# Weights kept split in DRAM: staging high and low parts in one layer and recalling them in the next, on one Trainium2 core

## The chip, the cores and the metric

The kernel runs on one core of a Trainium2 chip. The metric is the device time of one execution in microseconds, the median of several executions. The engines are TensorE (PE in the profile; PEld is its weight load), VectorE (DVE), ScalarE (ACT), GpSimd (POOL) and SyncE (SP), which here only issues DMA transfers. Each engine takes its instructions in the order of the program and waits on semaphores for the others. A queue of DMA issues is in order too: an issue that waits holds up those behind it.

## The reference

A decoder trunk of two layers on x of 1024 tokens by 1024 channels, in float32. Layer 0 is a gated pooling mixer, layer 1 a gated sliding-window attention that reads one shared K/V.

```python
for l in range(DEPTH):                                   # DEPTH = 2, N_A = 1
    shift, scale, gate = jnp.split(c_act @ ada_w[l] + ada_b[l], 3, axis=-1)
    if l < N_A:
        h = modulate(rmsnorm(x, norm_g[l]), shift, scale)
        y = pool_mixer(h, a_w_in[l], a_w_group[l], a_scale[l], a_w_out[l])
    else:
        if l == N_A:
            kb, vb = shared_kv_blocks(x, c_act, kv_norm_g, kv_ada_w, kv_ada_b, w_kv)
        h = modulate(rmsnorm(x, norm_g[l]), shift, scale)
        y = swa_sink_mixer(h, kb, vb, pos_bias, mask, b_w_in[j], b_sinks[j], b_w_out[j])
    x = x + gate[:, None, :] * y
return rmsnorm(x, final_g)
```

`pool_mixer` is a projection to u and z, trailing means of u over 2, 4, 8 and 16 tokens, a grouped projection, a gate by silu(z), and the out projection `a_w_out`. `swa_sink_mixer` is a projection to queries and gates (`b_w_in`), attention in blocks of 128 tokens with sinks, a gate, and the out projection `b_w_out`.

## The kernel before

Channels lie on the 128 partitions and tokens along the free dimension, in two halves of 512 tokens (q = 0 and 1). To keep float32 accuracy each matrix product is three passes of TensorE in the rounded type float32r: each operand is split into a high part (the value rounded) and a low part (the value less the high part), and high by high, high by low and low by high are summed in PSUM. A weight tile has 128 x 1024 numbers (512 KB). To split one, SyncE loads it into `raw`, ScalarE casts it to `wh`, and VectorE subtracts to make `wl` (`fetch`, `split_w`, `load_w`, lines 119 to 134). `raw`, `wh` and `wl` are rings of two buffers, so a weight can be split while the one before it is in use, and not earlier.

Layer 0 ends with its out projection (lines 829 to 864): 16 steps through `order`, each with one weight tile of `wao[n, hf]`, which `half_w` loads and splits one step ahead. For n below `LATE` = 5 both token halves are done (48 matmuls a step, steps 0 to 9), for n of 5 to 7 only the first (24 matmuls, steps 10 to 15). Into the steps the program weaves work that has nothing to do with them: `ADA[i]` calls of `ada_step`, each of which loads 512 KB of `ada_rest` into a `tmp` buffer (a ring of three) and takes a dot product on VectorE (line 239). At the end of an n the `residual` (line 686) adds the product to x, and squares are summed (lines 191 and 195). In this part TensorE's order is that of the program; a list scheduler of the language sets the order of the other engines from its own estimates.

The second token half of n = 7, 6, 5 follows (`last_chunk`, line 868) in an order written out by due times (`at`), beside the norm and the modulation of layer 1 (`step_h`, `fold_l`) and the first keys and values. `get_raw`, `take_h` and `take_l` load and split the weights for n = 6 and 5 again, and `wkv` and `wb[0]`.

Layer 1 (from line 989) runs a list of items `specs`: `keys`, `values`, `queries`, `gates`, `out_part`, `out_quarter`. Each names its weight as its first element, and the loop at the end loads and splits the weight for the next item (`load_w`) before it runs the present one. A GEMM here is 24 matmuls. Attention (`attend`, line 1086) is woven in by a clock: scores on TensorE, the softmax on VectorE and ScalarE, transposes (line 1125), two masks by GpSimd (lines 1134 and 1137), and the product with the values `LAGS` = 6 us later. Every weight of `wkv`, `wb` and part 0 of `wbo` is loaded and split twice, once for each token half. Part 1 of `wbo` is also split by `load_last` into four tiles that stay for the last quarter items; its low parts come from GpSimd (line 1224).

Of the kernel before, what the change touches and what calls it, by code (L numbers as in the profile page):

```python
# [18 lines left out]
P = 128  # L19
# [27 lines left out]

ENDS = (0, 1, 3, 5, 7)
# [7 lines left out]
def trunk(ctx, tc, xT, c, pack, ada_first, ada_rest, wu0_in, wg0_in, wa, wg, wao, wkv,  # L56
# [9 lines left out]
    pp = ctx.enter_context(tc.tile_pool(name="psum", bufs=1, space=PSUM))  # L66

# [65 lines left out]
    def load_w(src):  # L133
        return split_w(*fetch(src))

# [82 lines left out]
    with ExitStack() as sa:  # L218
# [580 lines left out]
        with tc.manual_schedule(engines={ET.PE}):  # L799
# [37 lines left out]
            ws, outs = {}, {}  # L837
            ws[0, 0] = half_w(0, 0)
            gather(4, 5, 6, 7)
            for i, (n, hf) in enumerate(order):  # L840
                if i + 1 < len(order):
                    ws[order[i + 1]] = half_w(*order[i + 1])
                if i == 0:
                    gather(8, 9)
                    new_x()
                    again_x(0)
                    gather(10, 11, 12, 13)
                elif i < 8:
                    again_x(i)
# [5 lines left out]
                for _ in range(ADA[i]):  # L855
                    ada_step()
                if hf == 1:
# [4 lines left out]
            assert rest_at[0] == len(rest_cols)  # L862
# [78 lines left out]
        def get_raw(key, src):  # L941
            lraw[key] = fetch(src)[0]

        def take_h(key):
            w = (ws if isinstance(key, tuple) else got)[key] = [
                wp.tile([P, 1024], F32R, tag=t, name=t) for t in ("wh", "wl")]
            nc.scalar.copy(out=w[0], in_=lraw[key])

        def take_l(key):
            w = (ws if isinstance(key, tuple) else got)[key]  # L950
            nc.vector.tensor_sub(out=w[1], in0=lraw.pop(key), in1=w[0].bitcast(F32))

        lraw = {}
        NT = 12 * 0.2157
        nl = 4 * len(late)
        weights = ([((n, hf), wao[n, hf]) for n in late[1:] for hf in range(2)]
                   + [("wk", wkv[0]), ("wv", wkv[1]), ("wq", wb[0])])
        for i, (key, src) in enumerate(weights):
            t = NT * 2 * (i + 1)
# [54 lines left out]
    def keys(q, hk, ps=None):  # L1014
# [11 lines left out]
        return wkv[0], lambda w: gemm_steps(w, 0, hk, KT, done)  # L1026
# [3 lines left out]
    def values(q, hk, ps=None):  # L1030
# [5 lines left out]
        return wkv[1], lambda w: gemm_steps(w, 0, hk, KT, done)  # L1036
# [15 lines left out]
    def queries(q, r, j, h1):  # L1052
# [14 lines left out]
        return wb[2 * r + j], run  # L1067

    def gates(q, r, j, h1):
# [12 lines left out]
        return wb[8 + 2 * r + j], run  # L1082
# [83 lines left out]
    def out_part(q, part, n2):  # L1166
# [11 lines left out]
        return wbo[part, n2], run  # L1178
# [39 lines left out]
    def load_last():  # L1218

        raw = wp.tile([P, 1024], F32, tag="raw", name="raw")  # L1220
        nc.sync.dma_start(raw, wbo[1, len(last_w)])
        w = hp.tile([P, 2, T], F32R, tag="h", name="wo")
        nc.scalar.copy(out=w[:, 0, :], in_=raw)
        nc.gpsimd.tensor_sub(out=w[:, 1, :], in0=raw, in1=w[:, 0, :].bitcast(F32))
        last_w.append((w[:, 0, :], w[:, 1, :]))
# [103 lines left out]
    def woven(l, at):  # L1329

        r = []
        for i, x in enumerate(l):
            r.append(x)
            if i in at:
                r.append(bare(load_last))
        return r

# [16 lines left out]
        *woven(project_out(0, 1) + project_out(1, 0)[:2], (0, 2, 4, 6)),  # L1354
# [8 lines left out]
    with tc.manual_schedule(engines={mybir.EngineType.PE}):  # L1363
        srcs = [i for i, sp_ in enumerate(specs) if sp_[0] is not None]
        loaded = {srcs[0]: got["wq"]}
# [66 lines left out]
```

## Time and profile before

| what | value |
|---|---|
| median of 3 runs | 985.02 us (984.18 to 985.11) |
| profiled execution | 984.87 us |
| its span | 982.6 us |
| TensorE busy | 961.9 us, 98% |
| VectorE, ScalarE, GpSimd busy | 775.7, 458.1, 145.0 us |
| moved by DMA | 125.67 MB, mean 128 GB/s |
| HBM read, written | 111.22 MB, 13.63 MB |

The span runs from the first instruction to the last; the execution's own time is a little longer. A row of the groups reads: line, engine, operation, tile written <- tiles read, shapes and count, then busy us and mean ns of one, then the idle time of the engine just before and who ended it. A row of a window reads: from and to, its length, busy us and count of each engine, the TensorE clock granted (1.00 is full), the mean busy share of the 16 DMA engines, and GB/s.

### The profile page before, as it was taken

What the parts mean: (1) busy time and instruction counts of PE and PEld (TensorE: products, weight loads), DVE (VectorE), ACT (ScalarE), POOL (GpSimd) and SP (SyncE); (2) the same over time, 40 slices, a digit from 0 to 9 for tenths busy, and PEclk for the clock granted to TensorE, in tenths of its full rate; (3) what the DMA queues carried; (4) which work ended last, traced back from release to release, by engine and by line L of the source; (5) the groups of instructions that cost most, each with busy time, mean ns of one, the idle gap of its engine ahead of it and who ended that gap; (6) DMA issues with size and microseconds to landing.
All of it is one profiled execution on the core that took longest, in us unless ns stands there. A gap on an engine that the chain in (4) does not pass through costs nothing.

```text
span 982.6 us, 12696 instructions
## 1 busy us (share of the span) xinstructions
PE 961.9 (98%) x4538; PEld 801.2 (82%) x4538; DVE 775.7 (79%) x1411; ACT 458.1 (47%) x902; POOL 145.0 (15%) x173
## 2 busy tenths in 40 slices
PE   8999999999999999999999999999999999999996
PEld 6788888888888887888888888877888888887786
DVE  5897978677978699676782278599899878889985
ACT  6534434333433244551111145486677546566544
POOL 2100000000000000000000000052324313335723
PEclk9999999999999999999999999999999999999998
DMA  9453622264225411779861223222211221223222
GB/s 331 183 174 114 192 103 65 78 201 150 65 85 194 150 64 57 262 267 327 305 216 65 86 64 130 86 65 69 82 66 64 87 86 65 64 88 106 86 87 86
DMA packets 40625, 125.67 MB, mean 128 GB/s; under 512 B 4465, under 2 KB 6641, under 8 KB 40434
## 3 DMA queue, kind: packets, MB, share of 16 engines
q1 hardware_dynamic: 40416, 123.82, 37.6%
q10 hardware_dynamic: 146, 1.05, 0.3%
q8 instruction: 35, 0.57, 0.2%
q14 instruction: 28, 0.23, 0.1%
HBM read 111.22 MB, written 13.63 MB: 127 GB/s over the span
## 4 chain that ended last, share of the span: by engine, by line
PE 78%; DVE 16%; issue 2%; ACT 2%; POOL 1%; DMA 0%; POOLq 0%; DVEq 0%; SPq 0%; ACTq 0%
PE ps_d L214 14%; PE ps_S L214 9%; PE ps_d L636 9%; PE ps_d L203 6%; PE ps_d L204 6%; PE ps_d L205 6%; PE ps_S L636 4%; PE ps_o L214 4%; PE ps_tp L214 3%; DVE wl L123 2%; PE ps_d L374 2%; PE ps_o L636 2%; PE ps_tp L636 2%; DVE tmp L542 2%; PE ps_tp L1125 1%
## 5 line engine op out<-in xcount | busy, mean ns | idle before, releaser
L121 ACT CAST wh<-raw 128x1024 fp32r<-128x1024 f32 x73 | 76.5, 1048 | 101.4 <-PE ps_d L214 78.5
L123 DVE TENSOR_TENSOR wl<-raw,wh 128x1024 fp32r<-128x1024 f32 x73 | 94.2, 1290 | 26.7 <-ACT wh L121 22.8
L203 PE MATMUL ps_d<-hm,wh 128*128 128x512 f32 x288 | 113.8, 395 | 0.0
L205 PE MATMUL ps_d<-hm,wl 128*128 128x512 f32 x288 | 112.4, 390 | 0.3 <-DVE wl L123 0.3
L204 PE MATMUL ps_d<-hm,wh 128*128 128x512 f32 x288 | 112.4, 390 | 0.0
L239 DVE CUSTOM_DVE_ANT_0 tmp<-tmp,cact,pk 128x1024 f32<-128x1024 f32 x48 | 60.7, 1282 | 33.2 <-DMA tmp<-ada_rest 32.9
L214 PE MATMUL ps_d<-gh,wh 128*128 128x512 f32 x224 | 82.0, 389 | 0.0
L214 PE MATMUL ps_S<-gh,wh 128*128 128x512 f32 x192 | 64.5, 390 | 0.0
L205 PEld LDWEIGHTS ps_d<-hm,wl 128*128 128x128 f32 x288 | 54.1, 188 | 12.6 <-DVE wl L123 1.1
L636 PE MATMUL ps_d<-hs,ws 128*128 128x512 f32 x264 | 63.4, 389 | 0.0
L1115 ACT ACTIVATE pt<-pt,nm 128x129 f32<-128x129 f32 x128 | 50.2, 394 | 26.8 <-DVE nm L1111 24.6
L203 PEld LDWEIGHTS ps_d<-hm,wh 128*128 128x128 f32 x288 | 54.1, 188 | 10.2
L204 PEld LDWEIGHTS ps_d<-hm,wh 128*128 128x128 f32 x288 | 54.2, 188 | 10.0
L636 PEld LDWEIGHTS ps_d<-hs,ws 128*128 128x128 f32 x264 | 49.5, 188 | 10.3
L542 DVE TENSOR_TENSOR tmp<-tmp 128x1039 f32<-128x1039 f32 (+3 forms) x40 | 49.4, 1235 | 6.8 <-ACT tmp L672 5.7
L612 ACT CAST ws<-tw 128x512 fp32r<-128x512 f32 x44 | 26.8, 621 | 53.9 <-PE ps_tp L214 15.1
L636 PE MATMUL ps_d<-ha,ws 128*128 128x512 f32 x216 | 51.9, 389 | 0.0
L534 POOL MEMSET tmp<- 128x16 f32 x16 | 1.7, 111 | 331.4 <-DVE tmp L542 115.9
L214 PEld LDWEIGHTS ps_d<-gh,wh 128*128 128x128 f32 x224 | 42.1, 188 | 8.7
L636 PEld LDWEIGHTS ps_d<-ha,ws 128*128 128x128 f32 x216 | 40.5, 188 | 8.4
L147 POOL TENSOR_TENSOR rs<-v,mhalf 128x4 f32<-128x4 f32 (+1 forms) x7 | 8.2, 1164 | 241.6 <-DVE v L145 241.6
L214 PE MATMUL ps_d<-gh,wl 128*128 128x512 f32 x112 | 43.6, 389 | 0.0
(294 smaller groups left out, 2492.0 us busy)
## 6 DMA issues: line engine op xcount, KB each, us to landing
tmp<-ada_rest SPq DMA_DIRECT2D x48, 512.0 KB, 4.7
raw<-wb SPq DMA_DIRECT2D x32, 512.0 KB, 3.3
raw<-wa SPq DMA_DIRECT2D x28, 512.0 KB, 3.7
raw<-wao SPq DMA_DIRECT2D x20, 512.0 KB, 4.1
ad<-ada_first SPq DMA_DIRECT2D x16, 512.0 KB, 5.0
x<-xT SPq DMA_DIRECT2D x32, 256.0 KB, 5.9
raw<-wbo SPq DMA_DIRECT2D x16, 512.0 KB, 3.3
kept_g<-tmp SPq DMA_DIRECT2D x14, 512.0 KB, 2.9
```

What stands on the lines that cost most here:

```text
L121: nc.scalar.copy(out=wh, in_=raw)
L123: nc.vector.tensor_sub(out=wl, in0=raw, in1=wh.bitcast(F32))
L203: mm(ps, lh, acts(k, 0), start=k == 0, stop=False)
L204: mm(ps, lh, acts(k, 1), start=False, stop=False)
L205: mm(ps, ll, acts(k, 0), start=False, stop=k == n - 1)
L214: mm(p, lhs, acts(k, hl, q), start=start and k == 0 and s == 0, stop=stop and k == n - 1 and s == 2)
L239: nc.vector.tensor_tensor_reduce(out=raw, in0=raw, in1=ca, scale=0.5, scalar=pk[:, bcol:bcol + 1], op0=ALU.mult, op1=ALU.add, accum_out=ad ...
L374: mm(psu[i, q], w0[k // 2][:, k % 2, w, i * P:(i + 1) * P], block(k, q)[hl], start=k == 0 and s == 0, stop=k == KT - 1 and s == 2)
L542: nc.vector.tensor_add(out=nx[:, 2 * s - 1:], in0=cur[:, 2 * s - 1:], in1=cur[:, s - 1:PAD + T - s])
L612: nc.scalar.copy(out=ws[i][:, 0, :], in_=src)
L636: mm(ps, lhs, acts(k, hl), start=start and k == 0 and s == 0, stop=k == 3 and s == 2, skip_group_check=True)
L1115: nc.scalar.activation(pt[:, i, :P + 1], pt[:, i, :P + 1], AF.Exp, bias=nm[:, i:i + 1], scale=-1.0, accum_out=den[:, i:i + 1])
```

## The change

While the out projection of layer 0 runs, 18 weight tiles of layer 1 (both of `wkv`, all 16 of `wb`) are loaded into a `tmp` buffer and split there: the high part goes to one of two `stage` tiles (ScalarE), the low part back into the buffer (VectorE). `keep` then stores both parts to DRAM, through SyncE. `STAGED[i]` says how many are done in step i. The four late output weights (n = 5 and 6) are split as before and kept as well. From then on `recall` brings a pair back by two transfers that GpSimd issues, straight into tiles of the rounded type. `pair_tiles` takes the pair from the two `raw` buffers or one of the two `wh`, `wl` pairs in turn, so three pairs rotate, and items of layer 1 have their weight two items ahead. The eight `wbo` tiles are loaded and split once each by `load_out`, with part 0 kept for the second token half and part 1 held on chip; `load_last` and `woven` are gone, and two out items change places.

```diff
+STAGED = (0, 0, 0, 0, 0, 1, 2, 3, 3, 3, 1, 1, 1, 1, 1, 1)
...
+    kp = ctx.enter_context(tc.tile_pool(name="kept", bufs=1, space=bass.MemoryType.DRAM))
...
+    def keep(key, hi, lo):
+        kept_w[key] = [kp.tile([P, 1024], F32, name="kw") for _ in range(2)]
+        for dst, src in zip(kept_w[key], (hi, lo)):
+            nc.sync.dma_start(dst, src.bitcast(F32))
+    def pair_tiles():
+        tags = (("raw", "raw"), ("wh", "wl"), ("wh", "wl"))[turns[0] % 3]
+        turns[0] += 1
+        return [wp.tile([P, 1024], F32R, tag=t, name="w2") for t in tags]
+    def recall(key):
+        w = pair_tiles()
+        for dst, src in zip(w, kept_w[key]):
+            nc.gpsimd.dma_start(dst, src)
+        return w
...
+            staged = [("kv", i, wkv[i]) for i in range(2)] + [
+                ("b", i, wb[i]) for i in (0, 1, 8, 9, 2, 3, 10, 11, 4, 5, 12, 13, 6, 7, 14, 15)]
+            def stage():
+                name, i, src = staged.pop(0)
+                raw = tmp()[:, :1024]
+                nc.sync.dma_start(raw, src)
+                hi = stage_hi[len(staged) % 2].rearrange("p a c -> p (a c)")
+                nc.scalar.copy(out=hi, in_=raw)
+                lo = raw.bitcast(F32R)
+                nc.vector.tensor_sub(out=lo, in0=raw, in1=hi.bitcast(F32))
+                keep((name, i), hi, lo)
...
                     ws[order[i + 1]] = half_w(*order[i + 1])
+                    if LATE <= order[i + 1][0] < KT - 1:
+                        keep(order[i + 1], *ws[order[i + 1]])
...
                 for _ in range(ADA[i]):
                     ada_step()
+                for _ in range(STAGED[i]):
+                    stage()
...
-            at(t - 4 * NT + 1.31 if i > 1 else -1.0, get_raw, key, src)
-            at(t + 0.05, take_h, key)
-            at(t + 1.3, take_l, key)
+        for i, w in enumerate(weights):
+            at(NT * 2 * i + 0.05 if i else -1.0, get_w, *w)
...
+    def load_out(part, n2):
+        raw = bp.tile([P, 1024], F32, tag="raw1", name="raw1", bufs=2)
+        nc.sync.dma_start(raw, wbo[part, n2])
+        if part:
+            t = hp.tile([P, 2, T], F32R, tag="h", name="wo")
+            last_w.append((t[:, 0, :], t[:, 1, :]))
+            w = last_w[-1]
+        else:
+            w = pair_tiles()
+        nc.scalar.copy(out=w[0], in_=raw)
+        nc.vector.tensor_sub(out=w[1], in0=raw, in1=w[0].bitcast(F32))
+        if not part:
+            keep(("o", part, n2), *w)
+        return w
+    def load_any(key):
+        return recall(key) if key in kept_w else load_out(*key[1:])
...
-        *woven(project_out(0, 1) + project_out(1, 0)[:2], (0, 2, 4, 6)),
+        *project_out(1, 0)[:2],
+        *project_out(0, 1),
...
-                nxt = srcs.index(i) + 1
+                nxt = srcs.index(i) + 2
                 if nxt < len(srcs):
-                    loaded[srcs[nxt]] = load_w(specs[srcs[nxt]][0])
+                    loaded[srcs[nxt]] = load_any(specs[srcs[nxt]][0])
```

The order on SyncE in the out projection. `raw` is a weight of layer 0's out projection, `tmp` from `ada_rest` an ada step, `tmp` from `wb` a stage's load, `kw` a store of a kept part. Before, from the load for step 9 (`raw_3994`) to that for step 15 (`raw_4278`):

```order
L130 DMA raw_3994<-wao 128x1024
L253 DMA tmp_4125<-ada_rest 128x1024
L253 DMA tmp_4167<-ada_rest 128x1024
L253 DMA tmp_4200<-ada_rest 128x1024
L253 DMA tmp_4238<-ada_rest 128x1024
L253 DMA tmp_4271<-ada_rest 128x1024
L130 DMA raw_4062<-wao 128x1024
L130 DMA raw_4136<-wao 128x1024
L130 DMA raw_4170<-wao 128x1024
L130 DMA raw_4207<-wao 128x1024
L130 DMA raw_4241<-wao 128x1024
L130 DMA raw_4278<-wao 128x1024
```

Now, the last 12 of the 19 rows from behind the load for step 12 to that for step 13 (`raw_4335`):

```order
L869 DMA tmp_4278<-wb 128x1024
L145 DMA kw_4228<-stage_3842 128x1024
L145 DMA kw_4229<-tmp_4224 128x1024
L145 DMA kw_4246<-wh_4242 128x1024
L145 DMA kw_4247<-wl_4244 128x1024
L145 DMA kw_4282<-stage_3843 128x1024
L145 DMA kw_4283<-tmp_4278 128x1024
L145 DMA kw_4292<-wh_4288 128x1024
L145 DMA kw_4293<-wl_4290 128x1024
L276 DMA tmp_4320<-ada_rest 128x1024
L869 DMA tmp_4323<-wb 128x1024
L133 DMA raw_4335<-wao 128x1024
```

The weight loads for the last steps stood side by side behind the last ada step; now stage loads, stores and ada steps stand between each two of them.

The order on VectorE at the end of the out projection: `wl` is the low part of a step's weight, `x` a residual, `sqh` the sum of squares, `tmp,adac` a dot, `tmp` with `stage` the low part of a staged weight. Before, from the residual at the end of step 11 (`ps_S_4142`) on, with the weights for steps 13, 14 and 15:

```order
L686 SCALAR_TENSOR_TENSOR x_3426<-ps_S_4142,adac_110,x_3426 128x512
L123 TENSOR_TENSOR wl_4211<-raw_4207,wh_4209 128x1024
L195 TENSOR_TENSOR sqh_3628<-sqh_3628,sq_4204 128x512
L123 TENSOR_TENSOR wl_4245<-raw_4241,wh_4243 128x1024
L686 SCALAR_TENSOR_TENSOR x_3427<-ps_d_4213,adac_110,x_3427 128x512
L123 TENSOR_TENSOR wl_4282<-raw_4278,wh_4280 128x1024
```

Now, from the same residual (`ps_S_4250`), with the weight for step 12 (`wl_4290`):

```order
L709 SCALAR_TENSOR_TENSOR x_3428<-ps_S_4250,adac_112,x_3428 128x512
L262 ISA tmp_4202,adac_112<-tmp_4202,cact_121,pk_75 128x1024
L262 ISA adac_112 128x1
L218 TENSOR_TENSOR sqh_3630<-sqh_3630,sq_4332 128x512
L262 ISA tmp_4205,adac_112<-tmp_4205,cact_121,pk_75 128x1024
L262 ISA adac_112 128x1
L873 TENSOR_TENSOR tmp_4208<-tmp_4208,stage_3842 128x1024
L126 TENSOR_TENSOR wl_4290<-raw_4286,wh_4288 128x1024
L873 TENSOR_TENSOR tmp_4216<-tmp_4216,stage_3843 128x1024
L873 TENSOR_TENSOR tmp_4224<-tmp_4224,stage_3842 128x1024
```

The split for step 13 stood behind the residual of step 11, and now that for step 12 stands there, with dots and a stage's subtraction ahead of it. Behind these rows come a dot, a stage, a dot and a stage, and then the split for step 13; the residual of step 13 and one stage more stand ahead of the split for step 14.

More of the change, by code (lines that the diff above doesn't have):

```diff
@@ L856, in trunk @@
                     ada_step()
+                if STAGED[i] and not stage_hi:
+                    stage_hi += [slot("stage") for _ in range(2)]
+                for _ in range(STAGED[i]):
+                    stage()
                 if hf == 1:
@@ L1177, in run @@
                 yield from gemm_steps(w, i * 512, acts, 4, done)
-        return wbo[part, n2], run
+        return ("o", part, n2), run
     def bare(f):
```

46 lines of the change are left out of this document (12 added, 34 removed).

## The prediction

> **What bounds the kernel now.** I read the page's parts 1 and 2 first. They show the share of each engine and the 40 slices of the span, 24.6 us each.
>
> ```profile
> span 982.6 us, 12696 instructions
> PE 961.9 (98%) x4538; PEld 801.2 (82%) x4538; DVE 775.7 (79%) x1411; ACT 458.1 (47%) x902; POOL 145.0 (15%) x173
> PE   8999999999999999999999999999999999999996
> DVE  5897978677978699676782278599899878889985
> DMA  9453622264225411779861223222211221223222
> GB/s 331 183 174 114 192 103 65 78 201 150 65 85 194 150 64 57 262 267 327 305 216 65 86 64 130 86 65 69 82 66 64 87 86 65 64 88 106 86 87 86
> ```
>
> TensorE is busy in every slice but the first and the last, so an engine relieved of work pays only where TensorE stands idle now, and any new wait of TensorE is paid in full. The DMA row has room in most places, but not in slices 16 to 19 (393 to 491 us). The stretches around the edit, in us of busy time, come next.
>
> ```profile
> core 0: us, PE busy (x) PEld busy (x) DVE busy (x) ACT busy (x) POOL busy (x), PEclk, DMA share, GB/s
> 439.00:507.00 68.00, 68.00 (x302) 56.31 (x301) 46.88 (x72) 10.13 (x12) 0.00 (x0) 1.00 0.88 299
> 507.00:565.00 58.00, 58.00 (x258) 48.02 (x257) 20.40 (x26) 11.06 (x13) 0.00 (x0) 1.00 0.26 87
> 565.00:640.00 75.00, 74.73 (x358) 62.58 (x357) 55.04 (x93) 36.88 (x63) 4.74 (x6) 1.00 0.28 92
> 640.00:700.00 60.00, 56.21 (x282) 46.54 (x281) 55.89 (x124) 45.85 (x98) 25.68 (x23) 1.00 0.20 64
> 700.00:975.00 275.00, 270.50 (x1433) 230.34 (x1432) 236.92 (x569) 164.72 (x403) 103.15 (x100) 1.00 0.25 81
> 975.00:982.60 7.60, 1.22 (x4) 0.93 (x4) 2.74 (x8) 0.00 (x0) 0.57 (x1) 0.50 0.39 138
> ...
> 5.00:20.00 15.00, 14.78 (x52) 10.57 (x53) 9.85 (x11) 8.81 (x14) 4.64 (x4) 1.00 1.01 362
> ```
>
> From 439 to 565 us TensorE does not idle at all. From 565 to 975 it idles for 0.27 + 3.79 + 4.50 = 8.6 us, and this is all that layer 1 can give back. The waits of TensorE say whom it waits for there, and the groups from 565 us on say what the change takes off those engines.
>
> ```profile
> PE ps_tp L1125 <- DVE pt L1119: 6.1, 5, 1.6
> ...
> L123 DVE TENSOR_TENSOR wl<-raw,wh 128x1024 fp32r<-128x1024 f32 x45 | 60.0, 1334 | 12.2 <-ACT wh L121 9.9 <-PE ps_o L1149 1.7
> L121 ACT CAST wh<-raw 128x1024 fp32r<-128x1024 f32 x45 | 47.0, 1045 | 15.2 <-issue 7.6 <-PE ps_d L204 6.4 <-ACT qt L1062 0.9
> L1134 POOL TENSOR_SCALAR_AFFINE_SELECT prev<-cur 128x1024 fp32r<-128x1024 f32 x28 | 33.3, 1189 | 46.8 <-DVE cur L1129 46.8
> ```
>
> **The gain in layer 1.** Of the 45 splits after 565 us, the eight of wbo stay as loads with a split. The other 37 lose 37 x 1.045 = 38.7 us of ScalarE and 37 x 1.334 = 49.4 us of VectorE. The five softmax waits for VectorE (6.1 us) are the target. At least 0 us is gained if VectorE's other work still arrives late, at most the 8.6 us of idle time. I take 5.0 us, nearer to the 6.1 us of the waits than to the end at nothing, because the wbo splits remain in the final stage. The four split writes of `load_last` that leave GpSimd are worth nothing: its queue has 103 us of work in 275.
>
> **What stages the pairs: the out projection of layer 0.** Its 16 steps start at 423.7 us. Ten steps have 48 matmuls and six have 24.
>
> ```profile
> L214 PE MATMUL ps_o<-gh,wh x64: 389/389/389, 423.7 to 531.6; 128*128 128x512 f32 x64
> 559.01 0.62 PE L214 MATMUL ps_S<-gh,wh 128*128 128x512 f32 x2
> 559.46 0.39 PE L214 MATMUL ps_S<-gh,wl 128*128 128x512 f32 x1
> 559.69 0.62 PE L214 MATMUL ps_S<-gh,wh 128*128 128x512 f32 x2
> ...
> 438.78 0.33 SPq L130 DMA_DIRECT2D raw<-wao  x1
> 507.47 49.42 SPq L130 DMA_DIRECT2D raw<-wao  x8
> ...
> tmp<-ada_rest SPq DMA_DIRECT2D x48, 512.0 KB, 4.7
> raw<-wb SPq DMA_DIRECT2D x32, 512.0 KB, 3.3
> tmp<-kept_g SPq DMA_DIRECT2D x5, 512.0 KB, 5.8
> ```
>
> Three matmuls start every 0.68 us (559.01 to 559.69), 0.227 us each: a step is 10.9 or 5.44 us. So TensorE starts step 12 at 543.4, step 13 at 548.8, step 14 at 554.2 and step 15 at 559.7 us. SyncE issues the load for step 4 at 438.78 us.
>
> Now I count SyncE's transfers in units of 512 KB (0.524 MB), from the load for step 4 up to and with that for step 15. Before: 12 weight loads, 30 of ada_rest and eight halves of x, 46 units. The loads for steps 10 to 15 stood last and alone. After: the same 46, plus 16 stage loads, 30 stage stores and 8 stores of late pairs, 100 units. The queue is in order, and the changed rows have the weight loads scattered between: the cumulative count is 55 at the load for step 11, 69 for step 12, 88 for 13, 95 for 14 and 100 for 15.
>
> At what rate do they go? The two busiest slices moved 331 and 327 GB/s; I take their mean, 329, because both held such long queues of loads: 1.594 us a unit. Its ends: 362 (window 5 to 20 us, share 1.01) and 299 (439 to 507 us, share 0.88, which has the same three-deep ring of tmp buffers). A unit alone lands 3.3 us after issue, so 1.7 us come on top of its 1.6. The split that follows is on ScalarE and VectorE, whose durations in this stage are these.
>
> ```profile
> L121 ACT CAST wh<-raw 128x1024 fp32r<-128x1024 f32 x13 | 13.7, 1055 | 86.2 <-PE ps_d L214 78.5 <-PE ps_S L214 7.7
> L239 DVE CUSTOM_DVE_ANT_0 tmp<-tmp,cact,pk 128x1024 f32<-128x1024 f32 x30 | 37.9, 1283 | 22.8 <-DMA tmp<-ada_rest 22.6
> L123 DVE TENSOR_TENSOR wl<-raw,wh 128x1024 fp32r<-128x1024 f32 x13 | 15.9, 1220 | 12.9 <-ACT wh L121 12.7
> L195 DVE TENSOR_TENSOR sqh<-sqh,sq 128x512 f32<-128x512 f32 x10 | 6.5, 684 | 0.0
> L239 DVE DVE_READ_ACCUMULATOR2_ANT adac<- 128x1 f32 x30 | 2.5, 82 | 0.0
> L191 ACT ACTIVATE sq<-x 128x512 f32<-128x512 f32 x10 | 6.3, 634 | 9.2 <-DVE x L686 8.9
> L686 DVE SCALAR_TENSOR_TENSOR x<-ps_S,adac,x 128x512 f32<-128x512 f32 x3 | 2.2, 749 | 3.3 <-PE ps_S L214 3.3
> ```
>
> In ScalarE's row the split waits 78.5 us for TensorE: the data lie ready and the buffer is what is missing. That is the cover, and this change uses it up. A weight is ready 1.7 + 1.06 + 1.22 = 4.0 us after its turn in the queue. At 329 GB/s:
> step 11: 438.8 + 55 x 1.594 + 4.0 = 530.5, needed at 537.9, in time.
> Step 12: 438.8 + 69 x 1.594 + 4.0 = 552.8, needed at 543.4: TensorE waits 9.4 us.
> Step 13: 583.1; TensorE is free at 552.8 + 5.4 = 558.2: 24.9 us.
> Step 14: 594.2, free at 588.5: 5.7 us. Step 15: 602.2, free at 599.6: 2.6 us.
> Sum 42.6 us. Only step 15 sets it: at 362 GB/s (1.448 us a unit) it is ready at 587.6, 27.9 us late; at 299 (1.753) at 618.1, 58.4 us late.
>
> The added waits on SyncE push the same way. Each store waits for ScalarE's cast or VectorE's subtraction, and the weight load stands behind it; a stage holds its tmp buffer through load, split and store, where an ada step holds it for load and dot. I charge them nothing beyond the rate, since the queue is full either way; they argue against 362. The extra work on ScalarE (18 casts, 19 us) and VectorE (18 subtractions, 22 us) lies in stretches in which VectorE has 37.6 us free after 507 us, so it costs no throughput, but its order does (rival C).
>
> After a stall TensorE may run slow: in the last window, with long pauses, the clock is 0.50. Between nothing and one pass at half speed (5.4 us more in step 15; the earlier ones hide behind the next load) I take nothing, since every other window reads 1.00.
>
> **The recalls.** GpSimd issues 44 pairs. The trace has no transfer from this queue. A pair's buffers come free when the weight three before is finished, two GEMMs or 10.9 us ahead of need. From below a pair costs one landing, 3.3 us; from above, for both together, the slowest median of a 512 KB load (5.8) behind two selects of GpSimd (2 x 1.19): 8.2 us. Nearest is the 5.8 us, since two transfers share the engines; all lie under 10.9, so I charge 0. Without that cover each microsecond over costs up to 44 us in all. The stores of wbo's part 0 (8 units) and the last stages (8 units after step 15) fall where the DMA share is 0.20 to 0.28, and cost nothing. Of a recall that waits for TensorE, GpSimd's selects behind it are queued; TensorE's use of those lies a lag of about 6 us later by the kernel's own table.
>
> **Sum.** The profiled execution took 984.87 us (its span 982.6 and 2.3 around it), 0.15 below the median of 985.02. 984.87 + 42.6 - 5.0 = 1022.5 us.
>
> **The rivals.**
> A, the forecast: 27.9 to 58.4 us of stalls, less 8.6 to 0 us: 1004 to 1043 us. Chance 0.70.
> B, recalls that land late, on top of A. For it: a queue that no row shows, a new kind of write into the rounded type, and a DMA load twice as large in layer 1. Against it: 81 GB/s in that stage, so doubled 162. It decides when a pair takes over 10.9 us; at 12 us, 44 x 1.1 = 48 us more, 1071 us. Chance 0.13.
> The Trainium skill speaks for it: "SBUF — State Buffer", section "SBUF: two separate sides", its box on the "DVE blocks DMA" trap says that GpSimd's cores write the descriptors of such a transfer and cannot do so while VectorE holds the port pair that both share, in copies above all. By that page's section "Who interferes with whom", a subtraction of two tensors, VectorE's main work here, has no such mode; no run so far shows either.
> C, the DMA engines are faster than every row and VectorE's order alone stalls TensorE. Ahead of the low part for step 12 now stand a residual that waits for the end of step 11, two dots with their accumulator reads of 82 ns, an add and a stage: 0.75 + 2 x 1.37 + 0.68 + 1.22 + 1.22 = 6.6 us, less the two matmuls that need only the high part, 0.45: 6.15. For step 13, five subtractions and two dots, 8.8 us, against 5.4 us of matmuls: 3.4. For step 14, residual, square, add, stage and split after the end of step 13: 4.5 - 0.45 = 4.05. Sum 13.6, so 984.87 + 13.6 - 5.0 = 993.5 us. Chance 0.10.
> The Trainium skill gives a ceiling for that: "DMA: Bandwidth & Descriptors", section "Where 436 GB/s comes from", 435 GB/s; by it the load for step 15 would be 3.6 us late (estimate from that page), and C would hold. The trace's 362 stands against it.
> D, the other side: the low-share stretch after 507 us takes the staging and no weight comes late. For it: 58 us at 0.26. Against it: the 54 units more are 28.3 MB, and 58 us x (329 - 87) GB/s has room for 14.0. It decides if the queue reaches step 15 by 555.7 us, 449 GB/s. Then 984.87 - 5.0 = 979.9 us. Chance 0.05.
> E, C without the 4.05 us of step 14, and the whole idle time of layer 1 gained: 984.87 + 9.55 - 8.6 = 985.8 us, no change. Chance 0.02.
>
> **How the numbers follow.** 0.2% is about what a measurement of this kernel can tell from no change. Faster is D, 0.05; same is E, 0.02; slower is A, B and C, 0.93. The time is A's. The range runs from C's 993 to 1050, past A's 1043 by the half-speed pass and rounding; it leaves out D, E and most of B, 0.18 or so.
>
> **What the changed profile would show.** Right: four idle stretches of TensorE between 543 and 605 us, before the first matmuls of steps 12 to 15, the largest at step 13; DMA share at 0.9 from 424 to past 600 us; the softmax waits of layer 1 mostly gone. Wrong if the DMA engines pass 400 GB/s through the stores, if TensorE idles in the middle of layer 1's GEMMs for a recalled pair, or if the weight loads leave SyncE as early as before.

## The result and the profile after

The changed kernel takes 1035.08 us (median of 5 runs, 1033.75 to 1039.28) against 985.11 us of the kernel before on the same chip: a ratio of 1.0507, 95% interval 1.0484 to 1.0531. The profiled execution took 1035.08 us, its span 1033.4. The page of the changed kernel, part 1 and the slices (now 25.8 us each):

```profile
PE 977.4 (95%) x4538; PEld 811.9 (79%) x4538; DVE 740.2 (72%) x1385; ACT 432.5 (42%) x872; POOL 174.2 (17%) x257
PE   8999999999999999999993399998999999999896
DMA  9444421452154116798998875734445544352022
```

In balance VectorE and ScalarE have 35.5 and 25.6 us less work, and TensorE has two slices at 3 tenths. Those slices (542 to 594 us) are the out projection's end, where the DMA row stands at 8 tenths. In stretches:

```profile
core 0: us, PE busy (x) PEld busy (x) DVE busy (x) ACT busy (x) POOL busy (x), PEclk, DMA share, GB/s
424.00:507.00 83.00, 83.00 (x368) 68.73 (x367) 53.09 (x76) 24.32 (x33) 0.00 (x0) 1.00 0.88 315
507.00:543.00 36.00, 36.00 (x161) 29.80 (x160) 20.62 (x26) 10.16 (x12) 0.00 (x0) 1.00 0.94 353
543.00:565.00 22.00, 9.82 (x29) 6.73 (x27) 12.45 (x17) 5.86 (x6) 0.00 (x0) 0.77 0.88 331
565.00:620.00 55.00, 34.54 (x123) 26.82 (x124) 19.02 (x23) 10.80 (x13) 4.39 (x5) 0.72 0.84 317
```

TensorE idles 12.2 us from 543 to 565 and 20.5 us from 565 to 620 us, and its clock falls to 0.77 and 0.72. TensorE's waits follow for two stretches: the out projection and the first of the last chunks (424 to 620 us), and behind the dots layer 1:

```profile
PE ps_d L237 <- ACT wh L124: 27.4, 2, 18.6
PE ps_S L237 <- ACT wh L124: 3.4, 1, 3.4
PE ps_o L165 <- DVE sqh L218: 1.1, 1, 1.1
PE ps_S L237 <- DVE wl L126: 0.7, 1, 0.7
...
PE ps_tp L1156 <- DVE pt L1150: 4.8, 3, 2.7
PE ps_o L165 <- POOL sqh L218: 4.4, 1, 4.4
```

Which part of the program lost how much is read from one instruction that both kernels have 128 times, the first product of the scores in layer 1: from its first start back lies layer 0, from its first to its last start layer 1. Kernel before, then the changed one:

```profile
L1105 PE MATMUL ps_S<-KH,qt x128: 220/282/368, 626.2 to 931.6; 128*128 128x256 f32 x112, 128*128 128x128 f32 x16
```

```profile
L1136 PE MATMUL ps_S<-KH,qt x128: 220/282/563, 671.3 to 983.1; 128*128 128x256 f32 x112, 128*128 128x128 f32 x16
```

The first score comes 45.1 us later, 0.5 of which stood before the out projection began. Layer 1 between the two is 311.8 us long instead of 305.4, 6.4 us more. Behind the last score 0.7 us are saved, which makes the 50.8 us of the spans. (Kernels that share the layer 0 of the kernel before reach the first score at 625.9 to 628.3 us in the traces below, and this difference already stands before the out projection. So the length from first to last score is the better measure of layer 1 in what follows.)

**The out projection, step by step.** The weight loads for steps 12 to 15 on SyncE, and ScalarE's cast of the one for step 12:

```profile
546.89 0.43 SPq L133 DMA_DIRECT2D raw<-wao  x1
572.64 0.45 SPq L133 DMA_DIRECT2D raw<-wao  x1
583.04 1.16 SPq L133 DMA_DIRECT2D raw<-wao  x1
593.57 0.71 SPq L133 DMA_DIRECT2D raw<-wao  x1
...
551.73 1.04 ACT L124 CAST wh<-raw 128x1024 fp32r<-128x1024 f32 x1 [0.35 <-DMA raw<-wao]
```

In the kernel before, the splits waited for TensorE (78.5 us). This one waits for its load. TensorE's rows where steps 12, 13 and 14 start:

```profile
552.82 1.22 PE L237 MATMUL ps_d<-gh,wh 128*128 128x512 f32 x2 [8.81 <-ACT wh L124]
...
554.68 1.05 PE L237 MATMUL ps_d<-gh,wh 128*128 128x512 f32 x2
555.53 0.63 PE L237 MATMUL ps_d<-gh,wl 128*128 128x512 f32 x1
...
559.45 0.62 PE L237 MATMUL ps_d<-gh,wh 128*128 128x512 f32 x2
559.91 0.40 PE L237 MATMUL ps_d<-gh,wl 128*128 128x512 f32 x1
...
580.22 1.22 PE L237 MATMUL ps_d<-gh,wh 128*128 128x512 f32 x2 [18.55 <-ACT wh L124]
...
592.40 0.73 PE L237 MATMUL ps_S<-gh,wh 128*128 128x512 f32 x2 [3.39 <-ACT wh L124]
```

The waits of 8.8 and 18.6 us end with the cast of a weight whose load came late: ScalarE stood idle until the load had landed (0.35 us of idle time in the cast's row at 551.73). Behind the first wait two matmuls take 0.85 us (554.68 to 555.53), and at 559.45 us again 0.46, which is the pace of before. The other waits are followed by the same slow pace.

The wait of 3.4 us at step 14 is of another kind. The landing of its load, which was issued at 583.04 us, and what ScalarE did then:

```profile
raw<-wao SPq DMA_DIRECT2D x1, 512.0 KB, 6.2
...
589.84 0.63 ACT L214 ACTIVATE sq<-x 128x512 f32<-128x512 f32 x1 [9.67 <-DVE x L709]
590.38 1.03 ACT L871 CAST stage<-tmp 128x1024 fp32r<-128x1024 f32 x1
591.31 1.04 ACT L124 CAST wh<-raw 128x1024 fp32r<-128x1024 f32 x1
```

The load landed at 589.2 us, 0.2 us after TensorE had finished step 13 (589.0). But ahead of the cast stood a square, which waited for the residual of step 13, and a stage's cast. With this order on ScalarE an earlier load would have changed nothing.

**Layer 1.** Two places in the changed kernel. VectorE and GpSimd at 696 us (L200: norm multiplications; L1149, L1150: softmax; L190 on GpSimd: low parts of the modulation), with TensorE's transposes that wait:

```profile
696.32 4.07 DVE L200 TENSOR_TENSOR xn<-x,rb 128x512 f32<-128x512 f32 x3
700.32 0.16 DVE L1149 RECIPROCAL den<-den 128x4 f32<-128x4 f32 x1
...
696.24 3.00 POOL L190 TENSOR_TENSOR hm<-xn,hm 128x512 fp32r<-128x512 f32 x2
...
702.06 0.80 PE L1156 MATMUL ps_tp<-ident,pt 128*128 128x128 f32 x4 [2.69 <-DVE pt L1150]
```

And at 967 us, residual, square, add and the statistics that TensorE takes from them:

```profile
969.03 0.74 DVE L709 SCALAR_TENSOR_TENSOR x<-ps_d,adac,x 128x512 f32<-128x512 f32 x1
...
969.94 0.61 ACT L214 ACTIVATE sq<-x 128x512 f32<-128x512 f32 x1
...
970.63 1.45 POOL L218 TENSOR_TENSOR sqh<-sqh,sq 128x512 f32<-128x512 f32 x1 [1.67 <-ACT sq L214]
...
972.14 1.87 PE L165 MATMUL ps_o<-invd,sqh 128*128 128x1 f32 x8 [4.38 <-POOL sqh L218]
```

The freed time of VectorE was filled with the next norm, three multiplications of which now stand ahead of a softmax's reciprocal. Beside GpSimd's subtractions these three take 4.07 us, where one alone takes 0.68 (experiment 7 comes back to this). And at 967 us the statistics follow directly on the item that they need.

### The profile page after: what moved, and what is told of

It is laid out like the page before. It is cut to its first block, busy times and chain, and to the rows that moved or that the text cites. A ratio compares the mean times of both kernels' runs of the same rounds, so it can differ in the third digit from the quotient of the medians.

```text
span 1033.4 us, 12803 instructions
## 1 busy us (share of the span) xinstructions
PE 977.4 (95%) x4538; PEld 811.9 (79%) x4538; DVE 740.2 (72%) x1385; ACT 432.5 (42%) x872; POOL 174.2 (17%) x257
## 4 chain that ended last, share of the span: by engine, by line
PE 70%; DVE 11%; DMA 11%; ACT 3%; issue 3%; SPq 2%; POOL 1%; POOLq 0%; DVEq 0%; ACTq 0%
PE ps_d L659 8%; PE ps_d L226 8%; PE ps_d L227 8%; PE ps_d L228 8%; PE ps_d L237 8%; PE ps_S L237 6%; DMA tmp<-ada_rest 4%; PE ps_S L659 4%; PE ps_d L397 2%; PE ps_o L659 2%; PE ps_tp L237 2%; PE ps_tp L659 2%; DMA tmp<-wb 2%; DVE tmp L565 2%; PE ps_o L237 2%
## 5 line engine op out<-in xcount | busy, mean ns | idle before, releaser
L226 PE MATMUL ps_d<-hm,w 128*128 128x512 f32 x288 | 114.1, 396 | 0.0
L227 PE MATMUL ps_d<-hm,w 128*128 128x512 f32 x288 | 112.6, 391 | 0.0
L228 PE MATMUL ps_d<-hm,w 128*128 128x512 f32 x288 | 112.5, 391 | 0.0
L237 PE MATMUL ps_d<-gh,wh 128*128 128x512 f32 x192 | 76.4, 413 | 27.4 <-ACT wh L124 27.4
L156 POOL DMA_DIRECT2D w<-kw x88 | 47.7, 543 | 322.5 <-DMA kw<-stage 223.4
L237 PEld LDWEIGHTS ps_d<-gh,wh 128*128 128x128 f32 x192 | 38.6, 202 | 36.3 <-ACT wh L124 28.2
L228 PEld LDWEIGHTS ps_d<-hm,w 128*128 128x128 f32 x288 | 54.2, 188 | 11.7
L226 PEld LDWEIGHTS ps_d<-hm,w 128*128 128x128 f32 x288 | 54.4, 189 | 10.2
L227 PEld LDWEIGHTS ps_d<-hm,w 128*128 128x128 f32 x288 | 54.4, 189 | 10.0
L237 PE MATMUL ps_S<-gh,wh 128*128 128x512 f32 x160 | 57.6, 410 | 3.4 <-ACT wh L124 3.4
L871 ACT CAST stage<-tmp 128x1024 fp32r<-128x1024 f32 x18 | 18.9, 1048 | 64.4 <-DMA tmp<-wb 35.2
L1186 DVE SCALAR_TENSOR_TENSOR of<-ps_o,ol 64x256 f32<-64x256 f32 x64 | 26.6, 416 | 25.8 <-ACT ol L1182 25.2
L124 ACT CAST wh<-raw 128x1024 fp32r<-128x1024 f32 x28 | 29.4, 1051 | 34.9 <-PE ps_d L237 25.3
```

The source lines that it names most:

```text
L124: nc.scalar.copy(out=wh, in_=raw)
L156: nc.gpsimd.dma_start(dst, src)
L226: mm(ps, lh, acts(k, 0), start=k == 0, stop=False)
L227: mm(ps, lh, acts(k, 1), start=False, stop=False)
L228: mm(ps, ll, acts(k, 0), start=False, stop=k == n - 1)
L237: mm(p, lhs, acts(k, hl, q), start=start and k == 0 and s == 0, stop=stop and k == n - 1 and s == 2)
```

## The experiments

Eleven kernels were run. Where not said otherwise the edit is to the changed kernel.

**1. Is it the staging's transfers or its splits?** First the transfers alone:

```diff
-                hi = stage_hi[len(staged) % 2].rearrange("p a c -> p (a c)")
-                nc.scalar.copy(out=hi, in_=raw)
-                lo = raw.bitcast(F32R)
-                nc.vector.tensor_sub(out=lo, in0=raw, in1=hi.bitcast(F32))
-                keep((name, i), hi, lo)
+                keep((name, i), raw, raw)
```

> The stages of layer 0 keep their loads and stores and lose their splits: the raw weight is stored twice, so layer 1 multiplies wrong low parts in the same time. In the changed kernel TensorE waits 32 us in all at the starts of steps 12, 13 and 14. Theory A (the weight loads stand behind the staging's transfers in SyncE's queue, 1.585 us a unit of 512 KB): the waits stay, 27 to 36 us in all. In this order the count of units is 76 at the load for step 11, 83 at 12, 90 at 13, 97 at 14 and 100 at 15, so the first long wait moves to step 11 (load lands at 438.9 + 76 x 1.585 + 1.7 = 561, needed at 538: about 24 us), and the time stays at 1030 to 1040 us. Theory C (the stages' subtractions on VectorE and casts on ScalarE stand ahead of the weight's split): without them no wait over 1 us between 424 and 605 us, and about 1035 - 43 = 992 us.

1030.79 us (1028.06 to 1032.8), ratio 1.0455 (1.0435 to 1.0475). The waits from 424 to 620 us:

```profile
PE ps_S L237 <- ACT wh L124: 25.4, 2, 22.8
PE ps_d L237 <- ACT wh L124: 5.3, 2, 2.8
PE ps_d L237 <- DVE wl L126: 0.9, 2, 0.5
```

31.8 us with a last row of 0.2, and the longest moved to step 11 with 22.8 us (about 24 expected). Without one split of the staging the loss is there (44.9 us against the kernel before).

Then the splits alone, with the loads and stores gone and the recalls reading the weights as they are:

```diff
-                nc.sync.dma_start(raw, src)
...
-                nc.scalar.copy(out=hi, in_=raw)
+                nc.scalar.copy(out=hi, in_=cact)
...
-                nc.vector.tensor_sub(out=lo, in0=raw, in1=hi.bitcast(F32))
-                keep((name, i), hi, lo)
+                nc.vector.tensor_sub(out=lo, in0=cact, in1=hi.bitcast(F32))
+                kept_w[name, i] = [src, src]
...
-                        keep(order[i + 1], *ws[order[i + 1]])
+                        kept_w[order[i + 1]] = [wao[order[i + 1]]] * 2
```

> The other half: the stages keep their cast and subtraction (of another tile, so they wait for no load) and lose their loads and stores, as do the late pairs' stores; layer 1 recalls the unsplit weights from where they lie in DRAM, the same bytes in the same order. VectorE's order is not the same as in the changed kernel, since the stages no longer wait for a load. Theory A: SyncE's queue holds the 46 units of before, so no wait of TensorE over 1 us between 424 and 605 us; the time is 1035 - 43 to 45 = 990 to 992 us, since layer 1 stays as in the changed kernel. Theory C: waits of about 13 us in steps 12 to 14 remain, about 1004 us.

990.31 us (989.42 to 992.5), ratio 1.005 (1.0035 to 1.0065). No wait of TensorE is listed between 424 and 620 us. The stretch that idled 12.2 us, and the scores:

```profile
543.00:565.00 22.00, 22.00 (x99) 18.22 (x98) 6.38 (x7) 4.35 (x5) 1.31 (x2) 1.00 0.24 73
...
L1135 PE MATMUL ps_S<-KH,qt x128: 220/282/562, 626.2 to 937.7; 128*128 128x256 f32 x112, 128*128 128x128 f32 x16
```

The first score is back at 626.2 us, to the tenth that of before; the loss of layer 1 stays (311.5 us). So the transfers cost the 45 us, and the 18 casts and 18 subtractions by themselves nothing. VectorE's order is another here, so this run does not show what the changed kernel's own order would cost with faster transfers; the first one shows that it isn't needed for the loss.

**2. The queue or the volume?** The stages' transfers go to GpSimd's queue:

```diff
-                nc.sync.dma_start(raw, src)
+                nc.gpsimd.dma_start(raw, src)
...
-                keep((name, i), hi, lo)
+                keep((name, i), hi, lo, nc.gpsimd)
```

> The stages' loads and stores are issued by GpSimd, which is idle there, and not by SyncE; the same bytes and splits. If the in-order queue alone holds the weight loads back, they now stand behind 46 to 50 units on SyncE and land after a shared transfer of 6 to 8 us: waits of 0 to 10 us in steps 11 to 15, 1035 - 32 to 43, that is 992 to 1006 us. If it is the volume (16 engines full, and the ring of three tmp buffers that ada steps and stages share, so that an ada load ahead of a weight load still waits for a stage's store), the waits stay at 20 us or more and the time at 1020 us or more.

1029.31 us (1028.13 to 1030.9), ratio 1.0438 (1.0421 to 1.0456): a queue of their own gives back 6 of 50 us. What SyncE's queue waits for most from 470 to 600 us, the longest of TensorE's waits from 424 to 620, and the engines from 543 to 565:

```profile
SPq L276 <- DMA kw<-tmp: 39.5, 8, 10.2
...
PE ps_S L237 <- DVE wl L126: 9.0, 3, 6.5
...
543.00:565.00 22.00, 15.49 (x61) 12.31 (x60) 12.84 (x17) 6.09 (x7) 3.90 (x8) 0.84 0.98 374
```

Ada loads, which stand ahead of weight loads on SyncE, now wait 39.5 us for stores from `tmp` buffers on the other queue: the ring of three ties the queues together, and the DMA engines are full (0.98). TensorE's waits come to 26.9 us, and 16.2 of them end with the low part of a weight on VectorE; in the two longest of these (6.5 and 3.9 us) dots stand ahead of it that wait for such ada loads. How the loss divides between ring, volume and VectorE's order was not separated.

**3. Half the dose.** Nine weights are staged, and the others are split and kept at their first use in layer 1 (by the `load_first` of experiment 6); the late items are those of experiment 4:

```diff
-STAGED = (0, 0, 0, 0, 0, 1, 2, 3, 3, 3, 1, 1, 1, 1, 1, 1)
+STAGED = (0, 0, 0, 0, 0, 1, 2, 3, 3, 0, 0, 0, 0, 0, 0, 0)
```

> Half the dose: 9 of 18 weights are staged, in steps 5 to 8; the other 9 are split and kept at their first use in layer 1; late items in the order of the run with the later sums of squares. The count of units is 71 at the load for step 12, 73 at 13, 79 at 14, 81 at 15. Theory A, by 1.585 us a unit: step 12's weight is ready at 438.9 + 71 x 1.585 + 2.7 = 554.1 us, needed at 543.9: one wait of 10 us (8 to 12), a slow start behind it of 3 us, none over 2 us in steps 13 to 15; 983 + 13 = 996 us, 994 to 999. Rival (a cost in proportion to the units added, 43 us for 54): 35 units give 28 us, 1011 us.

999.56 us (996.54 to 1002.21), ratio 1.0144 (1.0119 to 1.017), 0.6 us above the band. The waits from 424 to 620 us are one row:

```profile
PE ps_d L237 <- ACT wh L124: 9.8, 1, 9.8
```

One wait of 9.8 us where 10 was worked out, and none behind it. Two thirds of the added units (35 of 54) cost a third of the waits (9.8 of 31.5 us). What counts is how many units stand ahead of the load that is needed next, beyond the slack.

**4. The late items.** The statistics one item later:

```diff
-        stats(0), project_out(1, 0)[2], finish(0, 4, FINISH[0]),
-        *project_out(1, 0)[3:],
+        project_out(1, 0)[2], stats(0), project_out(1, 0)[3], finish(0, 4, FINISH[0]),
+        *project_out(1, 0)[4:],
```

> Only the order of three items late in layer 1 is changed: the sums of squares of the first token half (stats) are taken one output item later, and so is the last norm of that half; layer 0 is that of the changed kernel. There TensorE waits 4.4 us at 967 us for the chain residual, square, add that follows the last output item, and then runs about 14 matmuls at half pace. Theory: the changed order of the output items took away the item that stood between, and this puts one there again: the wait goes, 5 to 7 us less, 1028 to 1030 us. Rival: the add on GpSimd is late because recalls and selects stand ahead of it on GpSimd's queue; then the wait only moves with it, and the time stays within 1.5 us of 1035.

1026.24 us (1022.22 to 1029.89), ratio 1.041 (1.0378 to 1.0442), 8.8 us less than the changed kernel, more than expected. The wait of 4.4 us for `sqh` is gone from the list, and the scores show

```profile
L1136 PE MATMUL ps_S<-KH,qt x128: 220/282/562, 669.6 to 972.7; 128*128 128x256 f32 x112, 128*128 128x128 f32 x16
```

303.1 us of layer 1 instead of 311.8, now 2.3 less than before. Its profiled execution was also 1.7 us earlier at the first score, which the edit does not touch. Recalls on GpSimd had no part in this wait: in the changed kernel GpSimd stood idle for 1.67 us before the add, until the square was done (row at 970.63).

**5. What the idea is worth if staging is free.** Nothing staged, recalls of unsplit weights, late items as in 4:

```diff
+            for name, i, src in staged:
+                kept_w[name, i] = [src, src]
...
-                for _ in range(STAGED[i]):
-                    stage()
...
-                        keep(order[i + 1], *ws[order[i + 1]])
+                        kept_w[order[i + 1]] = [wao[order[i + 1]]] * 2
```

> What layer 1 would gain if the staging cost nothing: nothing is staged or kept in layer 0, and the recalls bring the unsplit weights, the same bytes in the same order (the low parts are then wrong); the order of the late items is that of the run with the later sums of squares. Theory (layer 1 can give back little, since the freed engines' time is filled by the next norm's multiplications): from the two earlier runs TensorE was ahead of the kernel before by 0.7 us before the late items and by 2.2 us more through them: 985.9 - 2.9 = 983.0 us, 982 to 984. Rival (the five softmax waits of 6.1 us all go, as the prediction took it, and the cover gives its 2.2 us beside): 978 us.

981.26 us (978.53 to 983.12) against 985.01, ratio 0.9959 (0.9943 to 0.9975): 3.7 us gained, just below the 982 to 984 expected and far from the rival's 978.

```profile
L1124 PE MATMUL ps_S<-KH,qt x128: 220/282/365, 628.3 to 930.2; 128*128 128x256 f32 x112, 128*128 128x128 f32 x16
```

Layer 1 is 301.9 us long, 3.5 less than before. More than that the 37 casts and 37 subtractions are not worth there, and part of it belongs to the late items (experiment 6 has a control for these).

**6. Without staging: split at first use, keep, recall in the second half.** On top of 4 (`stage` is gone, the last chunks of layer 0 are those of the kernel before, with `keep` behind the splits of `wkv` and `wb[0]`):

```diff
+    def load_first(key):
+        raw = bp.tile([P, 1024], F32, tag="raw1", name="raw1", bufs=2)
+        nc.sync.dma_start(raw, wbo[key[1:]] if key[0] == "o" else wb[key[1]])
...
+        w = pair_tiles()
+        nc.scalar.copy(out=w[0], in_=raw)
+        nc.vector.tensor_sub(out=w[1], in0=raw, in1=w[0].bitcast(F32))
+        keep(key, *w)
...
+    def load_any(key):
+        return recall(key) if key in kept_w else load_first(key)
```

> A whole version without staging: the weights of layer 1 are loaded and split at their first use there (first token half), as before, then stored as a pair by SyncE, and recalled by GpSimd for the second half; the late output weights of layer 0 are treated as in the kernel before; the late items in the order of the run with the later sums of squares. 18 splits are saved in place of 37, with 36 stores of 512 KB in the first half of layer 1, where the DMA share was 0.20 to 0.25. Theory (the late waits are in the second half, and the DMA engines have room there): 982 to 984.5 us. Rival (stores and recalls in layer 1 delay the weights, or splits in the first half keep all its waits and the gain is lost in it): 985.5 us or more.

990.5 us (989.1 to 992.02), ratio 1.0054 (1.0038 to 1.0071): the theory missed. VectorE and GpSimd at 670 us of this run:

```profile
669.90 4.66 DVE L200 TENSOR_TENSOR xn<-x,rb 128x512 f32<-128x512 f32 x1
...
669.84 1.10 POOL L1163 TENSOR_SCALAR_AFFINE_SELECT cur<-cur 128x1024 fp32r<-128x1024 f32 x1
670.88 0.55 POOL L156 DMA_DIRECT2D w<-kw  x1
671.44 2.56 POOL L190 TENSOR_TENSOR hm<-xn,hm 128x512 fp32r<-128x512 f32 x2
```

A multiplication of 0.68 us takes 4.66. It starts just after GpSimd's select, and ends at 674.56, 0.56 us after the last of GpSimd's instructions (671.44 + 2.56 = 674.0). Meanwhile the softmax behind it waits.

A mend, built on the kernel before, keeps the first half's order (loads one item ahead, keys and values split twice) and keeps only `wb` and part 0 of `wbo`:

```diff
+        w = load_w(wbo[key[1:]] if key[0] == "o" else (wkv if key[0] == "kv" else wb)[key[1]])
+        if key[0] != "kv":
+            keep(key, *w)
+        return w
```

> The version without staging once more, with the first half of layer 1 left as in the kernel before (weights loaded and split one item ahead; keys and values split twice): only the 16 tiles of wb and part 0 of wbo are stored as pairs behind their first split, and recalled for the second half, two items ahead; late items in the order of the run with the later sums of squares. VectorE's order up to the second half is that of before. Theory (in the run before this one the first half lost 8 us to norm multiplications that moved ahead of the softmax, and the second half gained 2.4): no loss, 2 to 3 us gained, 985.0 - 2.5 = 982.5 us, 981.5 to 984. Rival (36 stores and 40 recalls cost in layer 1 by themselves): 985 us or more.

982.75 us (981.07 to 984.19) against 985.75, ratio 0.997 (0.9958 to 0.9982), as expected: 3.0 us faster than before, 52 faster than the changed kernel. This lies within 0.5% of no change, but the interval excludes 1. The control has the same late items and no `keep`:

```diff
-        if key[0] != "kv":
-            keep(key, *w)
```

> The control for it: the same kernel without the stores and recalls, so each weight of wb and of part 0 of wbo is loaded and split twice as in the kernel before; the late items and the loads of part 1 of wbo stay in the new order. If the gain comes from the order of the late items alone: the same time as with recalls, 982 to 983.5 us. If it comes from the splits saved in the second half: 984.5 to 986 us.

983.88 us (982.79 to 986.59), ratio 0.9986 (0.9977 to 0.9995). It lies between the two readings: by the medians 1.9 us of the 3.0 come with the late items alone (1.4 by the ratio). What the saved splits add beyond that lies within the overlap of the intervals and stays open. Their scores, the version with recalls first:

```profile
L1131 PE MATMUL ps_S<-KH,qt x128: 220/282/365, 628.3 to 932.0; 128*128 128x256 f32 x112, 128*128 128x128 f32 x16
```

```profile
L1131 PE MATMUL ps_S<-KH,qt x128: 220/282/365, 625.9 to 930.5; 128*128 128x256 f32 x112, 128*128 128x128 f32 x16
```

303.7 and 304.6 us, against 305.4.

**7. Does GpSimd block VectorE?** The eight subtractions L190 of the first modulation go to VectorE, in the version that lost (6) and in its mend:

```diff
-                m.step(k)
+                m.step_h(k)
+                m.step_l(k, nc.vector if m is hk1 else None)
```

> On top of the first version without staging (990.5 us, the one that lost 8.8 us early in layer 1): the low parts of the second half's first modulation (hm, 8 subtractions of 1.29 us on GpSimd) go to VectorE. There a multiplication of the norm on VectorE (two inputs in SBUF) took 1.77 to 4.66 us in place of 0.68 whenever GpSimd was in such a subtraction, a select or behind one another. Theory (VectorE was blocked by GpSimd's instructions): no multiplication over 1 us beside a subtraction, the early loss falls from 8.8 to under 4 us, 982.5 to 986 us. Rival (the order of VectorE's work, or its load: 8 x 0.69 = 5.5 us more lie on it): 990 us or more.

> The same edit on top of the version that was 3.0 us faster than before (982.75 us; its first half stands in the order of before, 4 of 13 multiplications stretched to 0.9 to 1.8 us, softmax waits 5.3 us in four). Theory of the block: the stretched ones cost 3.2 us of VectorE, and the edit gives it 5.5 us more work, so about even: 981 to 984 us. Rival (the softmax waits come from the block alone): 978 to 980 us.

In the one that lost: 985.97 us (983.93 to 987.91), ratio 1.0005 (0.9995 to 1.0015), 4.5 us back of the 7.8 that lie between it and its mend.

```profile
L200 DVE TENSOR_TENSOR xn<-x,rb x16: 657/684/1755, 644.5 to 740.5; 128x512 f32<-128x512 f32 x16
```

The longest multiplication fell from 4.66 to 1.76 us, and that one stands beside a select. In the mend: 986.48 us (985.18 to 987.17), ratio 1.0008 (0.9999 to 1.0017), 3.7 us lost where about even was expected (1.8 us by first and last score, 305.5 us in place of 303.7). No multiplication was over 0.69 us there. That the 5.5 us of work that VectorE took over made other things late is likely, and was not tested by itself. The block is shown; whether the edit pays depends on the order: it gained in the first version and lost in the mend.

## Why the prediction was right, and where not

**What sets the time: right.** The out projection's weight loads come late behind the staging's transfers, at steps 12 and 13 as named. The count of 100 units at 1.594 us gave step 15's load its turn at 598.2 us. By the trace the load landed at 599.0 us; less the 1.7 us of landing and from the load for step 4 at 438.9, that is 158.4 us for 100 units, 1.584 us each, 331 GB/s. This is the pace of the queue and not that of the DMA engines: in five microseconds the engines moved 419 GB/s (565 to 570 us, DMA share 1.03) or 211 (590 to 595, 0.57), and from 424 to 600 us SyncE waited, among other things,

```profile
SPq L145 <- ACT stage L871: 30.3, 14, 6.6
```

30.3 us with stores for the stages' casts. The text had charged such waits "nothing beyond the rate"; that its 329 GB/s, taken from slices of loads, came out as the mean of faster stretches and such pauses was in part luck.

**Step 12: 9.4 us forecast, 8.8 measured. Step 13: 24.9 and 18.6. Step 14: 5.7 and 3.4 + 0.7. Step 15: 2.6 and 0.** The first matmuls came at 552.8, 580.2 and 592.4 us against 552.8, 583.1 and 594.2. At step 13 the weight was 2.9 us earlier than forecast (1.2 of them are the low part, which the first two matmuls do not need), and TensorE came 3.5 us later to it, because of its slow pace. At step 14 the time is near, but the cause is not the one of the forecast: the queue's 5.7 us were replaced by the chain of rival C, residual, square, stage and split after the end of step 13, which C had priced at 4.05 us. Measured are 4.1. Three idle stretches stand there in place of four.

**The sum: 42.6 us forecast, 44.6 measured (45.1 less the 0.5 at the start).** The waits for weights fell 11 us short (31.5) and TensorE's pace made it up. The step that failed is "between nothing and one pass at half speed I take nothing": after each of the three waits some 14 matmuls ran at half pace, about 3 us more each time. Up to step 15 this took the place of waiting for the next load, as the text said: step 15 began at 601.8 us against 602.2, 0.4 us after its weight was ready. What was left came behind that start, 3.0 us: the wait of 1.1 us for the statistics and a slow stretch after it (613.6 to 617 us). The Trainium skill, "TensorE: Matmul & The Clock Gate", section "Part 1: The HAM clock gate (the "warmup" mystery)", has a window of about 3.4 us, after which an idle TensorE falls to half its clock and needs as much to come back; the pauses of 3.4 to 18.6 us here agree, with PEclk at 0.77 and 0.72, and the slow stretch behind the first, 552.8 to some 559 us, is nearly two such windows. Shorter slow stretches followed the waits of 1.1 us (at 611 us) and 2.7 us (at 702 us) too, which this window does not give.

**Layer 1: -5.0 us forecast, +6.4 measured. This step failed, and in sign.** Two mistakes. The change's "two out items change places" was told and not priced: it took the item away that covered residual, square and add, 4.4 us of waiting and a slow start behind it (experiment 4, 8.8 us in all). And "nearer to the 6.1 us of the waits" took freed time of VectorE for time that the softmax gets. The waits are still 4.8 us and not "mostly gone": in the longest, 2.7 us, the softmax stands behind three norm multiplications that the scheduler moved into the gap, and two of these took 1.76 and 1.79 us in place of 0.68 beside GpSimd. With the late items mended and staging free the gain is 3.7 us, within the 0 to 8.6 that were given.

**The recalls: right at nothing.** TensorE waits for no recalled tile in the lists above, and the page gives the landing as

```profile
w<-kw POOLq DMA_DIRECT2D x88, 512.0 KB, 4.2
```

4.2 us where 5.8 was taken. So rival B did not happen. Rival C, as the account of the whole loss, fell with experiment 1: the loss is there without the stages' subtractions. Its chain showed only at step 14. Rival D would have needed 449 GB/s and more on the mean, and E, like C, faster engines than any row; the windows of the staging moved 315 to 353. By the 435 GB/s of the Trainium skill that stood beside C ("DMA: Bandwidth & Descriptors", section "Where 436 GB/s comes from") C would have held. The same section gives some 358 GB/s as the limit of one core's HBM traffic, which the prediction left out; the 419 GB/s from 565 to 570 us lie above that, so the mean of 331 does not bear it out.

The forecast of 1022.5 us came out 12.6 us low. Of that 11.4 us are layer 1, 2.0 the out projection and 0.5 the start, less 0.7 behind the last score and 0.6 between execution time and span (2.3 us before, 1.7 now).

## What to carry to other kernels

Count what stands in the queue ahead of the next transfer that the bottleneck engine needs, and set its time against the date of need; transfers that "fit into the mean" cost nothing until the slack is used up, and then their full time (35 units 9.8 us, 54 units 31.5 us of waits). Of an edit that moves items, price each place where a chain's last link was covered by the item that moved. Work taken off an engine that was waited for is only worth what the scheduler does not fill with other work. And a wait that came out near its forecast is to be read for its cause as well: at step 14 it was another.

## What the runs showed of the hardware

A multiplication on VectorE with both inputs in SBUF (L200, 0.68 us) took 1.77 us beside one of GpSimd's subtractions, and 4.66 us when a select, a DMA issue and two subtractions of GpSimd followed one another without a gap: VectorE did not go on at half pace, it stood until GpSimd paused. The same is seen in the kernel before (three multiplications of 0.93 to 1.77 us) and in the changed one (three of 1.76 to 1.79); each of them ends 0.54 to 0.56 us after the end of an instruction of GpSimd. With GpSimd's subtractions gone the median stayed 0.68 and only the one beside a select was long (1.76). The Trainium skill, "SBUF — State Buffer", section "Who interferes with whom", says that such an instruction of VectorE contends with a GpSimd instruction that reads SBUF, by a lock for the whole instruction; the trace agrees, and adds that a row of GpSimd instructions can keep the lock. The prediction had used that section for GpSimd's transfers alone and had left this sentence out.

A DMA queue of GpSimd's own brought no more throughput to this kernel: from 439 to 599 us 325 GB/s were moved with two queues (DMA share 0.92) and 334 with one (0.90). Over 5 us both reached 419.
